# Convolution accumulators in four one-bank buffers, two convolution channels placed sooner, one convolution moved from GpSimd to TensorE, and whole low parts on GpSimd in the first FFN

## The chip, the cores and the metric

The kernel runs on one NeuronCore of one Trainium2 chip. Five engines with an instruction stream each work side by side: TensorE (PE; its weight loads are listed apart as PEld), VectorE (DVE), ScalarE (ACT), GpSimd (POOL) and SyncE (SP), which issues most of the DMAs. The metric is the time of one execution on the device in microseconds. Three executions of the kernel before took 1547.32 to 1551.12 us, with 1550.37 us as median.

## The reference

One step of a streaming encoder on 640 tokens: 512 frames of a new stream (the prompt) and 8 running streams with 16 frames each (the sample), width 1024. Layer 0 is a convolution module and a feed-forward network (FFN), layer 1 attention and an FFN. The change touches layer 0 only:

```python
def conv_module(h, hist, g, w_pw1, b_pw1, w_dw, b_dw, ln_g, ln_b, w_pw2, b_pw2):
    a, gate = jnp.split(rms_norm(h, g) @ w_pw1 + b_pw1, 2, axis=-1)
    glu = a * jax.nn.sigmoid(gate)
    full = jnp.concatenate([hist.astype(glu.dtype), glu], axis=1)
    y = lax.conv_general_dilated(
        full, w_dw[:, None, :].astype(full.dtype), window_strides=(1,), padding="VALID",
        dimension_numbers=("NWC", "WIO", "NWC"), feature_group_count=D_MODEL) + b_dw
    y = jax.nn.silu(layer_norm(y, ln_g, ln_b))
    return h + y @ w_pw2 + b_pw2, full[:, -CONV_HIST:]

def swiglu_ffn(h, g, w_in, w_out):
    a, b = jnp.split(rms_norm(h, g) @ w_in, 2, axis=-1)
    return h + (jax.nn.silu(a) * b) @ w_out
```

The convolution is depthwise and 31 wide; the FFN's hidden width is 2816. Everything is float32.

## The kernel before

**Layout.** Channels lie on the 128 partitions, in 8 tiles of 128 channels; below, "channel 6" is the seventh of these tiles. Tokens lie along the free axis, in two groups (`GR`, line 43): group 0 with 256 tokens (128 of the sample and 128 of the prompt) and group 1 with 384 of the prompt. Layer 0 works through the groups one after the other.

**Products.** A float32 product is made from three matmuls (`mm3`, lines 170 to 172): each operand is split into a high part that TensorE takes at full rate and a low part, the rest. `wsplit` (line 128) does it for weights: one DMA brings 128x2048 values to `raw`, ScalarE copies them to `whi` (line 150), and `wlo` = raw − whi is subtracted (line 154) by VectorE for the first columns and GpSimd for the last `pool` quarters of them. `raw`, `whi` and `wlo` have two buffers each, so the copy of one tile's weights waits until the tile two before it has been read by its last matmul. The same split of activations is `xsplit` (lines 159 and 160).

**The convolution** of one channel tile and group runs in one of three ways. `conv` (letter d in the plan): VectorE, 31 instructions (a start at line 434, 30 steps at line 437) that add into an accumulator in PSUM from the pool `w2`; each buffer of the pool spans two banks and holds two channels, and there are two buffers. `conv_pool` (letter q): ScalarE multiplies (line 416), GpSimd adds (line 417), 31 and 30 instructions. `conv_pe_load` and `conv_pe` (letters l and p): the input goes to DRAM and back four times shifted (DMAs sc and x4), and TensorE makes 32 small matmuls (line 469).

**The order.** `PLAN` (line 70) gives the order of the program for the convolution layer. Its letters, each with the group and the channels behind it: a and b are pw1 with the gate (b is group 1), x the norm of group 1, d, q, l and p convolutions, n the LayerNorm with the swish (`conv_ln`), w is pw2, r the norm ahead of the FFN, f one chunk of the FFN for group 0 (six tiles of `ffn_in`, then `ffn_out`), s the output of the convolution's state. From the program, a scheduler makes one list of instructions for each engine; blocks under `high_priority` are placed earlier than where they stand. Each engine then works through its list in that fixed order, and waits where an operand isn't ready. So an instruction that stands early in a list and must wait holds everything behind it.

**What the prediction follows.** n0 is a chain over four engines: sums over channels on GpSimd and TensorE (`colmean`), the mean to all partitions (`spread`, line 216), subtraction on VectorE (line 483), squares on ScalarE (line 179), their sums on GpSimd (line 195) and TensorE (line 204), `rst` (lines 226 and 230), spread, product (line 489), swish (line 491), split into x. Behind it stand pw2 of group 0, four weight tiles of two output tiles each (w0), then two more pw1 tiles, r0 and the FFN's first tiles. The FFN's tiles are called t0, t1, ... here.

Of the kernel before, what the change touches and what calls it, by code (L numbers as in the profile page):

```python
# [8 lines left out]
F32 = mybir.dt.float32  # L9
# [5 lines left out]
P = 128  # L15
# [33 lines left out]
HP = 2000  # L49
# [17 lines left out]
FG = (1, 0)  # L67
SSQ1 = 'ppapappp'
LNO = ((1, 5, 4, 3, 6, 0, 2, 7), (3, 5, 6, 4, 2, 7, 1, 0))
PLAN = ("a0 y a1 a2 a4 x a3 a5 a6 l04 p04 l05 d0213 a7 b0 p05 b1 l07 p07 l06 b2 q00 s0 p06 n0 b3 b4 b5 d145 l13 w0 b7 r0 p13 b6 f q16 s1 d101 d127 n1 f f w1 r1")  # L70
# [7 lines left out]
def tile_trunk(ctx, tc, xT, vecs, hist, w_pw1, w_pw2, w_in0, w_out0, w_in1, w_out1,  # L78
# [3 lines left out]
    cst = ctx.enter_context(tc.tile_pool(name="cst", bufs=1))  # L82
    wp = ctx.enter_context(tc.tile_pool(name="wp", bufs=2))
    w2s = ExitStack()
    w2 = w2s.enter_context(tc.tile_pool(name="w2", bufs=2, space=PSUM))

    uid = [0]
    tps = ExitStack()
# [3 lines left out]
    def nm(s):  # L92
        uid[0] += 1
        return f"{s}_{uid[0]}"
# [1 line left out]
    def mmt(n=512):  # L96
        return mm.tile([P, n], F32, tag="mm", name=nm("mm"))

    sums = [512]

    def w2t():
        return w2.tile([P, 1024 if sums[0] == 512 else 512], F32, tag="w2", name=nm("w2"))

    h = cst.tile([P, KT, NT], F32, name="h", tag="h")

# [67 lines left out]

    last = {}

    def square(s, n, eng="a"):
        q = tp.tile([P, 384], F32, tag="sq", name=nm("sq"))
        if eng == "a":
            nc.scalar.activation(out=q[:, :n], in_=s, func=AF.Square)  # L179
        else:  # L180
            e = nc.vector if eng == "v" else nc.gpsimd
            e.tensor_tensor(out=q[:, :n], in0=s, in1=s, op=ALU.mult)
        return q[:, :n]

    def colmean(st, pieces, n, cut, tag, eng=nc.gpsimd):
        nt = n // P
        srcs = []
        prev = acc = None
        for s in pieces[:cut]:
            if prev is None:  # L190
                prev = s()
                continue
            if acc is None:
                acc = tp.tile([P, 384], F32, tag="acc", name=nm("acc"))
            last["acc"] = eng.tensor_tensor(out=acc[:, :n], in0=prev, in1=s(), op=ALU.add)  # L195
            prev = acc[:, :n]
        if prev is not None:
            srcs.append(lambda: prev)
        srcs += pieces[cut:]
        w, c0 = len(srcs), sums[0]  # L200
        for k, f in enumerate(srcs):
            s = f()
            for t in range(nt):
                last["sum"] = nc.tensor.matmul(st[:, c0 + t * w + k:c0 + 1 + t * w + k], s[:, t * P:(t + 1) * P],
                                               onec, start=True, stop=True)
        r = tp.tile([P, 4], F32, tag=tag, name=nm(tag))
        if w > 1:
            nc.vector.tensor_reduce(out=r[:, :nt],
                                    in_=st[:, c0:c0 + nt * w].rearrange("p (t k) -> p t k", k=w),
                                    op=ALU.add, axis=mybir.AxisListType.X)  # L210
            return r, r[:, :nt]
        return r, st[:, c0:c0 + nt]
# [206 lines left out]

    def conv(cs, g):  # L420
        n = GR[g][1]
        sts = [w2t() for _ in range(0, len(cs), 2)]
        sts = [sts[i // 2][:, i % 2 * 512:i % 2 * 512 + n] for i in range(len(cs))]
        for j in range(W):
            for i, c in enumerate(cs):
                if g == 0:
                    src = gs[:, c, :, j:j + SB]
                    dst = sts[i].rearrange("p (s w) -> p s w", w=SB)
                else:
                    src = gp[:, c, j:j + n]  # L430
                    dst = sts[i]
                wj = dcol(V_DW + c * W + j)
                if j == 0:
                    nc.vector.tensor_scalar(out=dst, in0=src, scalar1=wj, scalar2=col(V_BDW, c),
                                            op0=ALU.mult, op1=ALU.add)
                else:
                    nc.vector.scalar_tensor_tensor(out=dst, in0=src, scalar=wj, in1=dst,  # L437
                                                   op0=ALU.mult, op1=ALU.add)
# [79 lines left out]
    def step(op, arg):  # L518
# [46 lines left out]

    xs = [rms_late(0, None), rms_late(1, None)]
    tps.close()
    at = ExitStack()
    aps = ExitStack()
    am = aps.enter_context(tc.tile_pool(name="am", bufs=2, space=PSUM))  # L570
    mm = aps.enter_context(tc.tile_pool(name="mm1", bufs=2, space=PSUM))

# [302 lines left out]
            proj_o(PO[p])  # L875
    sps.close()
    aps.close()
    w2s.close()
# [4 lines left out]
    sums[0] = 384  # L883
# [22 lines left out]
    def after(ins):  # L906
        return tc.issue_after(ins.ins) if ins is not None else ExitStack()

    def tmp(t):
        return tp.tile([P, 384], F32, tag=t, name=nm(t))[:, 0:HT]  # L910
# [361 lines left out]
```

## Time and profile before

| what | value |
|---|---|
| median of three runs | 1550.37 us |
| profiled execution | 1551.3 us, its span 1549.5 us |
| mean granted TensorE clock | 0.984 of full speed |
| moved by DMA | 199.95 MB, 129 GB/s |
| VectorE's first eight groups hold | wlo 214.0 us, convolution steps of 384 tokens 103.9 us |
| ScalarE's copies of weights (line 150) | 197.7 us |
| GpSimd's part of the low parts (line 154) | 145.7 us |

The profile shows one execution. Its page gives busy time by engine, the chain that ended last, and groups of instructions: line of the kernel, engine, operation, tile written and tiles read, count, then busy time and mean length in ns, then the idle time of the engine ahead of them and what ended it. Times in rows of the trace are microseconds from the start of the span.

### The profile page before, as it was taken

Reading aid. Unit: us, or ns where it says so; the run is one execution under the profiler, and the core shown is the slowest. Engines: PE = TensorE matmul, PEld = TensorE weight load, DVE = VectorE, ACT = ScalarE, POOL = GpSimd, SP = SyncE. Lnnn points to the kernel's source line nnn. Section 1 sums busy time; section 2 is a strip of 40 time slices with the busy share of each in tenths; the row PEclk is TensorE's granted clock in tenths of the full one; section 3 lists DMA queues with packets and bytes.
Section 4 is the critical chain, followed back from the end, with each engine's and each line's share of the span. In section 5 each row is a group of like instructions: output and inputs, shape, how many; then the busy total and the mean of one; then the engine's idle time right before and its main releaser. Section 6 shows DMA issues by size and latency. Waiting matters only on the chain.

```text
span 1549.5 us, 26569 instructions
## 1 busy us (share of the span) xinstructions
PE 1471.7 (95%) x10770; PEld 1398.9 (90%) x10770; DVE 1050.1 (68%) x1863; ACT 662.4 (43%) x1173; POOL 443.8 (29%) x403
## 2 busy tenths in 40 slices
PE   5888998989999999999999999999989999999997
PEld 5878888989999999999988798886989999999997
DVE  6994999988555455457576767566796476476455
ACT  4544454535423323235454445443554244244244
POOL 6865568877501000001321211110411121121110
PEclk9999999999999999999999999998999999999998
DMA  7784434444421333433655545453103213213211
GB/s 236 234 228 142 137 113 159 148 157 153 147 82 55 129 116 129 135 118 126 202 183 201 174 140 205 133 175 114 55 28 109 82 56 109 82 55 109 82 55 68
DMA packets 59658, 199.95 MB, mean 129 GB/s; under 512 B 10128, under 2 KB 22672, under 8 KB 46736
## 3 DMA queue, kind: packets, MB, share of 16 engines
q1 hardware_dynamic: 59248, 197.96, 39.1%
q8 instruction: 84, 1.38, 0.4%
q10 hardware_dynamic: 288, 0.31, 0.1%
q14 instruction: 38, 0.31, 0.1%
HBM read 187.02 MB, written 11.22 MB: 128 GB/s over the span
## 4 chain that ended last, share of the span: by engine, by line
PE 71%; DVE 16%; ACT 3%; issue 3%; DMA 3%; POOL 2%; SPq 0%; POOLq 0%; DVEq 0%; ACTq 0%
PE mm L170 12%; PE mm L172 12%; PE mm L171 12%; PE pb L968 6%; DVE w L437 5%; DVE wlo L154 4%; PE pc L968 4%; PE pa L968 4%; PE pb L170 1%; PE pb L171 1%; PE pb L172 1%; PE pa L172 1%; PE pa L170 1%; PE pc L170 1%; PE pc L172 1%
## 5 line engine op out<-in xcount | busy, mean ns | idle before, releaser
L171 PE MATMUL mm<-x,wlo 128*128 128x256 f32 (+1 forms) x1344 | 416.8, 312 | 15.4 <-DVE wlo L154 14.9
L170 PE MATMUL mm<-x,whi 128*128 128x256 f32 (+1 forms) x1344 | 413.3, 312 | 6.4 <-ACT x L159 3.7
L172 PE MATMUL mm<-x,whi 128*128 128x256 f32 (+1 forms) x1344 | 412.7, 311 | 0.5
L150 ACT ACTIVATE whi<-raw 128x2048 fp32r<-128x2048 f32 (+2 forms) x117 | 197.7, 1694 | 232.6 <-PE mm L172 138.8
L171 PEld LDWEIGHTS mm<-x,wlo 128*128 128x128 f32 x1344 | 257.1, 192 | 18.7 <-DVE wlo L154 17.5
L170 PEld LDWEIGHTS mm<-x,whi 128*128 128x128 f32 x1344 | 254.5, 191 | 11.2 <-ACT x L159 4.1
L172 PEld LDWEIGHTS mm<-x,whi 128*128 128x128 f32 x1344 | 255.1, 191 | 2.9 <-DVE x L160 1.8
L154 DVE TENSOR_TENSOR wlo<-raw,whi 128x2048 fp32r<-128x2048 f32 (+5 forms) x117 | 214.0, 1832 | 62.2 <-ACT whi L150 61.2
L154 POOL TENSOR_TENSOR wlo<-raw,whi 128x1536 fp32r<-128x1536 f32 (+3 forms) x50 | 145.7, 2918 | 69.0 <-ACT whi L150 69.0
L913 POOL TENSOR_TENSOR raw<-raw 128x512 f32<-128x512 f32 x38 | 50.5, 1330 | 332.3 <-DVE raw L913 257.5
L171 PE MATMUL mm<-hid,wlo 128*128 128x256 f32 (+1 forms) x352 | 107.7, 308 | 6.6 <-DVE wlo L154 6.6
L172 PE MATMUL mm<-hid,whi 128*128 128x256 f32 (+1 forms) x352 | 105.8, 307 | 0.2
L170 PE MATMUL mm<-hid,whi 128*128 128x256 f32 (+1 forms) x352 | 104.6, 307 | 0.1
L437 DVE SCALAR_TENSOR_TENSOR w<-gp,dwv,w 128x384 f32<-128x384 f32 x180 | 103.9, 612 | 0.8
L195 POOL TENSOR_TENSOR acc<-sq,sq 128x384 f32<-128x384 f32 (+1 forms) x8 | 8.1, 1006 | 258.2 <-ACT sq L179 258.1
L171 PEld LDWEIGHTS mm<-hid,wlo 128*128 128x128 f32 x352 | 66.0, 188 | 7.8 <-DVE wlo L154 7.8
L417 POOL TENSOR_TENSOR y<-y,cvt 128x256 f32<-128x256 f32 (+1 forms) x60 | 69.3, 1154 | 6.3 <-ACT cvt L416 4.0
L172 PEld LDWEIGHTS mm<-hid,whi 128*128 128x128 f32 x352 | 65.7, 188 | 0.6 <-DVE hid L160 0.6
L159 ACT ACTIVATE whi<-raw 128x1024 fp32r<-128x1024 f32 x38 | 39.4, 1054 | 61.6 <-PE pc L172 18.1
L170 PEld LDWEIGHTS mm<-hid,whi 128*128 128x128 f32 x352 | 65.2, 188 | 0.4 <-ACT hid L159 0.3
L968 PE MATMUL pa<-x0f,whi 128*128 128x320 f32 x228 | 61.2, 316 | 2.5 <-DVE t L913 2.3
L195 POOL TENSOR_TENSOR acc<-acc,sq 128x384 f32<-128x384 f32 (+1 forms) x48 | 52.7, 1097 | 28.9 <-ACT sq L179 27.5
(317 smaller groups left out, 3391.4 us busy)
## 6 DMA issues: line engine op xcount, KB each, us to landing
raw<-in_w_in SPq DMA_DIRECT2D x62, 1024.0 KB
raw<-in_w_out SPq DMA_DIRECT2D x36, 768.0 KB
raw<-in_w_pw SPq DMA_DIRECT2D x22, 1024.0 KB
cache<-in_ck SPq DMA_DIRECT2D x32, 512.0 KB
cache<-in_cv SPq DMA_DIRECT2D x32, 512.0 KB
raw<-in_w_kq SPq DMA_DIRECT2D x8, 1024.0 KB
x<-sc SPq DMA_DIRECT2D x16, 368.0 KB
raw<-in_w_out SPq DMA_DIRECT2D x4, 1024.0 KB
```

The costliest lines, as they stand in the source:

```text
L150: nc.scalar.activation(out=hi[:, a:b], in_=raw[:, a:b], func=AF.Copy)
L154: eng.tensor_tensor(out=lo[:, a:b], in0=raw[:, a:b], in1=hi[:, a:b].bitcast(F32), op=ALU.subtract)
L159: nc.scalar.activation(out=hi, in_=src, func=AF.Copy)
L170: nc.tensor.matmul(ps, wh, xh, start=(i == 0), stop=False)
L171: nc.tensor.matmul(ps, wl, xh, start=False, stop=False)
L172: nc.tensor.matmul(ps, wh, xl, start=False, stop=(i == last))
L195: last["acc"] = eng.tensor_tensor(out=acc[:, :n], in0=prev, in1=s(), op=ALU.add)
L417: nc.gpsimd.tensor_tensor(out=y[g][:, c, :], in0=y[g][:, c, :], in1=pr[:, :n], op=ALU.add)
L437: nc.vector.scalar_tensor_tensor(out=dst, in0=src, scalar=wj, in1=dst, op0=ALU.mult, op1=ALU.add)
L913: ENG[e].tensor_tensor(out=out, in0=a, in1=b, op=op)
L968: nc.tensor.matmul(ps, a[:, c], b[:, k, :], start=(first and k == 0 and i == 0), stop=(k == 3 and i == 2), skip_group_check=not first)
```

## The change

1. The pool `w2` gets four buffers of one bank (512 values) instead of two of two banks, so that each convolved channel has a buffer of its own. Small sums that lay in the second bank now lie at column 384 of the one bank. The pool is closed ahead of the attention, which opens its own of the old shape.
2. Channels 0 and 1 of group 1 (`d101`) are convolved ahead of n0 in the program, where they stood behind s1. Each block of VectorE's convolutions now issues its first instruction after the end of the block before (`issue_after`).
3. `conv_ln` runs under `high_priority`.
4. Channel 6 of group 1 goes from `conv_pool` (q16) to TensorE (l16, p16 around the first FFN chunk).
5. `ffn_in` gives GpSimd all 2048 columns of wlo where it had 1536 (`pool=3`, in the first three chunks); `ffn_out` there stays at three quarters, 1152 of 1536. The other chunks have pool 0 before and after.

```diff
-PLAN = ("... b2 q00 s0 p06 n0 b3 b4 b5 d145 l13 w0 b7 r0 p13 b6 f q16 s1 d101 d127 n1 f f w1 r1")
+PLAN = ("... b2 q00 s0 p06 d101 n0 b3 b4 b5 d145 l13 w0 b7 r0 p13 b6 l16 f p16 s1 d127 n1 f f w1 r1")
...
-    w2 = w2s.enter_context(tc.tile_pool(name="w2", bufs=2, space=PSUM))
+    w2 = w2s.enter_context(tc.tile_pool(name="w2", bufs=4, space=PSUM))
...
-    sums = [512]
+    wide_w2 = [512]
     def w2t():
-        return w2.tile([P, 1024 if sums[0] == 512 else 512], F32, tag="w2", name=nm("w2"))
+        return w2.tile([P, wide_w2[0]], F32, tag="w2", name=nm("w2"))
...
+    def after(ins):
+        return tc.issue_after(ins.ins) if ins is not None else ExitStack()
...
-        w, c0 = len(srcs), sums[0]
+        w, c0 = len(srcs), 384
...
-        wh, wl = wsplit(wsrc[j], 16, P, pool=pool)
+        wh, wl = wsplit(wsrc[j], 16, P, pool=4 if pool else 0)
...
-        sts = [w2t() for _ in range(0, len(cs), 2)]
-        sts = [sts[i // 2][:, i % 2 * 512:i % 2 * 512 + n] for i in range(len(cs))]
+        sts = [w2t()[:, 0:n] for _ in cs]
...
                 if j == 0:
-                    nc.vector.tensor_scalar(out=dst, in0=src, scalar1=wj, scalar2=col(V_BDW, c),
-                                            op0=ALU.mult, op1=ALU.add)
+                    with after(last.get("conv")):
+                        nc.vector.tensor_scalar(out=dst, in0=src, scalar1=wj,
+                                                scalar2=col(V_BDW, c), op0=ALU.mult,
+                                                op1=ALU.add)
...
+        last["conv"] = end
...
         elif op == "n":
-            zs[g] = conv_ln(g)
+            with tc.high_priority(offset=HP):
+                zs[g] = conv_ln(g)
```

The order moves at three places that the prediction speaks of. In the rows, the number behind a tile's name counts the tiles of the program. The first place is VectorE ahead of n0's `rst`. Before, from the subtraction of the mean (y) on; w_213 is a convolution of d145, gp the gated input that a pw1 tile leaves:

```order
L483 TENSOR_TENSOR y_106<-y_106,w_168_1345 128x256 x8
L395 SCALAR_TENSOR_TENSOR gp<-t_204_1562,t_205_1564 128x384
L154 TENSOR_TENSOR wlo_1704<-raw_1702,whi_1703 128x1024
L434 TENSOR_SCALAR w_213_1628<-gp,dwv,vec 128x384
L226 TENSOR_SCALAR rst_1397<-w_171_1370 128x2
```

And now, the last part of it; w_169 and w_170 are d101, whose steps alternate:

```order
L398 SCALAR_TENSOR_TENSOR gp<-t_214_1690,t_215_1692 128x384
L441 SCALAR_TENSOR_TENSOR w_170_1347<-gp,dwv,w_170_1347 128x384
L441 SCALAR_TENSOR_TENSOR w_169_1346<-gp,dwv,w_169_1346 128x384
L154 TENSOR_TENSOR wlo_1831<-raw_1829,whi_1830 128x1024
...
L229 TENSOR_SCALAR rst_1464<-w_174_1437 128x2
...
L494 TENSOR_TENSOR y_106<-y_106,w_174_1437 128x256 x8
```

At the first "..." stand six more steps of d101, at the second five. In all there are 22 steps between d101's two starts and the subtraction of the mean, 21 between that and rst, where there was one start of d145; with them a second gp and a second wlo moved ahead of rst. From rst to the last x tile of r0 VectorE's list has 77 steps and 4 starts, where it had 46 and 2.

The second place is GpSimd at the sums of n0's squares (acc and sq), before and now:

```order
L195 TENSOR_TENSOR acc_1373<-acc_1373,sq_1383 128x256
L154 TENSOR_TENSOR wlo_1704<-raw_1702,whi_1703 128x1024
L195 TENSOR_TENSOR acc_1373<-acc_1373,sq_1386 128x256
L195 TENSOR_TENSOR acc_1373<-acc_1373,sq_1389 128x256
L195 TENSOR_TENSOR acc_1373<-acc_1373,sq_1392 128x256
L230 TENSOR_TENSOR rst_182_1399<-rst_1397,mhalf 128x2
L154 TENSOR_TENSOR wlo_1763<-raw_1761,whi_1762 128x1024
```

```order
L198 TENSOR_TENSOR acc_1440<-acc_1440,sq_1453 128x256
L198 TENSOR_TENSOR acc_1440<-acc_1440,sq_1456 128x256
L154 TENSOR_TENSOR wlo_1831<-raw_1829,whi_1830 128x1024
L198 TENSOR_TENSOR acc_1440<-acc_1440,sq_1459 128x256
L233 TENSOR_TENSOR rst_185_1466<-rst_1464,mhalf 128x2
```

The low part of pw2's second weight tile stood behind rst, and stands ahead of the last add now. On ScalarE its copy, whi_1830, has moved ahead of the last square in the same way.

The third place is TensorE at the end of pw2's first two weight tiles. Before, mm_1709 and mm_1735 (the first tile's two outputs) end here, and mm_1768 (the second tile's) goes on behind them:

```order
L172 MATMUL mm_1709<-x_1403,whi_1703 128x256
L170 MATMUL mm_1735<-x_1403,whi_1703 128x256
L171 MATMUL mm_1735<-x_1403,wlo_1704 128x256
L172 MATMUL mm_1735<-x_1403,whi_1703 128x256
L170 MATMUL mm_1768<-x_1403,whi_1762 128x256
L171 MATMUL mm_1768<-x_1403,wlo_1763 128x256
```

And now; mm_1777 and mm_1803 are the first tile's outputs, mm_1836 and mm_1862 the second's, mm_1895 and mm_1921 the third's:

```order
L172 MATMUL mm_1777<-x_1470,whi_1771 128x256
L172 MATMUL mm_1803<-x_1470,whi_1771 128x256
L172 MATMUL mm_1836<-x_1470,whi_1830 128x256
L172 MATMUL mm_1862<-x_1470,whi_1830 128x256
L170 MATMUL mm_1895<-x_1470,whi_1889 128x256
L170 MATMUL mm_1921<-x_1470,whi_1889 128x256
L170 MATMUL mm_1954<-x_1470,whi_1948 128x256
```

The two weight tiles used to end one after the other, and now end together, by turns to the last x tile. The FFN's first two tiles, t0 and t1, which came one after the other, are interleaved in the same way; and the 32 matmuls of p16 stand at the end of the first chunk, 5 of them in its last output tiles and 27 behind these. No matmul stands between n0's last spread and pw2, before or now.

More of the change, by code (lines that the diff above doesn't have):

```diff
@@ L69 @@
 LNO = ((1, 5, 4, 3, 6, 0, 2, 7), (3, 5, 6, 4, 2, 7, 1, 0))
-PLAN = ("a0 y a1 a2 a4 x a3 a5 a6 l04 p04 l05 d0213 a7 b0 p05 b1 l07 p07 l06 b2 q00 s0 p06 n0 b3 b4 b5 d145 l13 w0 b7 r0 p13 b6 f q16 s1 d101 d127 n1 f f w1 r1")
+PLAN = ("a0 y a1 a2 a4 x a3 a5 a6 l04 p04 l05 d0213 a7 b0 p05 b1 l07 p07 l06 b2 q00 s0 p06 d101 n0 b3 b4 b5 d145 l13 w0 b7 r0 p13 b6 l16 f p16 s1 d127 n1 f f w1 r1")
 V_NCONV, V_BPW1, V_BDW, V_LNG, V_LNB, V_BPW2 = 0, 8, 24, 32, 40, 48
@@ L433, in conv @@
                 if j == 0:
-                    nc.vector.tensor_scalar(out=dst, in0=src, scalar1=wj, scalar2=col(V_BDW, c),
-                                            op0=ALU.mult, op1=ALU.add)
-                else:
-                    nc.vector.scalar_tensor_tensor(out=dst, in0=src, scalar=wj, in1=dst,
-                                                   op0=ALU.mult, op1=ALU.add)
+                    with after(last.get("conv")):
+                        nc.vector.tensor_scalar(out=dst, in0=src, scalar1=wj,
+                                                scalar2=col(V_BDW, c), op0=ALU.mult,
+                                                op1=ALU.add)
+                else:
+                    end = nc.vector.scalar_tensor_tensor(out=dst, in0=src, scalar=wj, in1=dst,
+                                                         op0=ALU.mult, op1=ALU.add)
+        last["conv"] = end
         for i, c in enumerate(cs):
@@ L567, in tile_trunk @@
     tps.close()
+    w2s.close()
     at = ExitStack()
     aps = ExitStack()
+    w2 = aps.enter_context(tc.tile_pool(name="w2a", bufs=2, space=PSUM))
+    wide_w2[0] = 1024
     am = aps.enter_context(tc.tile_pool(name="am", bufs=2, space=PSUM))
@@ L877, in tile_trunk @@
     aps.close()
-    w2s.close()
+    wide_w2[0] = 512
     hf = ExitStack()
@@ L882, in tile_trunk @@
     w2 = hf.enter_context(tc.tile_pool(name="w2f", bufs=2, space=PSUM, **tr))
-    sums[0] = 384
     mm = hf.enter_context(tc.tile_pool(name="mm2", bufs=2, space=PSUM, **tr))
@@ L904, in tile_trunk @@
     xp = hf.enter_context(tc.tile_pool(name="xp", bufs=1, **tr))
-    def after(ins):
-        return tc.issue_after(ins.ins) if ins is not None else ExitStack()
     def tmp(t):
```

## The prediction

> **What bounds the kernel now.** I read the head of the page first, then its chain, then TensorE's waits, then 20-us windows, and last single rows.
>
> ```profile
> PE 1471.7 (95%) x10770; PEld 1398.9 (90%) x10770; DVE 1050.1 (68%) x1863; ACT 662.4 (43%) x1173; POOL 443.8 (29%) x403
> PE 71%; DVE 16%; ACT 3%; issue 3%; DMA 3%; POOL 2%; SPq 0%; POOLq 0%; DVEq 0%; ACTq 0%
> L171 PE MATMUL mm<-x,wlo 128*128 128x256 f32 (+1 forms) x1344 | 416.8, 312 | 15.4 <-DVE wlo L154 14.9
> L417 POOL TENSOR_TENSOR y<-y,cvt 128x256 f32<-128x256 f32 (+1 forms) x60 | 69.3, 1154 | 6.3 <-ACT cvt L416 4.0
> ```
>
> TensorE is busy 95% of the span, so only its idle time of 1549.5 − 1471.7 = 77.8 us can be won, plus the time lost at half clock. The next view (TensorE's waits from 60 to 400 us, then busy time of each engine by window: PE, PEld, DVE, ACT, POOL, granted clock, DMA share, GB/s) shows where it sits.
>
> ```profile
> PE mm L171 <- DVE wlo L154: 21.6, 18, 3.6
> PE mm L469 <- DMA x<-sc: 10.5, 2, 5.4
> 120.00:140.00 20.00, 20.00 (x150) 19.07 (x143) 8.31 (x14) 6.42 (x12) 8.99 (x9) 1.00 0.45 130
> 140.00:160.00 20.00, 15.87 (x88) 15.13 (x87) 12.59 (x26) 12.99 (x22) 10.79 (x9) 0.83 0.40 141
> 160.00:180.00 20.00, 18.18 (x160) 17.98 (x159) 19.72 (x31) 10.04 (x14) 12.10 (x8) 1.00 0.31 106
> 200.00:220.00 20.00, 17.79 (x126) 17.39 (x125) 20.00 (x35) 10.94 (x19) 11.65 (x6) 0.91 0.29 66
> 400.00:1549.00 1149.00, 1126.16 (x8054) 1073.53 (x8053) 704.74 (x1325) 465.92 (x883) 162.83 (x192) 0.99 0.34 114
> ```
>
> After 400 us TensorE has 22.8 us idle in 1149, and the change leaves the work there as it is. All is decided before 400 us. There VectorE is nearly full from 160 us on, and has free time only in 120 to 160: 11.7 + 7.4 us. That is where the change puts d101, 2 × 31 instructions.
>
> **The change part by part.** *d101 ahead of n0.* First the durations, and the chain that starts pw2 of group 0 (start, length, engine, line; in brackets the idle time before and what ended it).
>
> ```profile
> 119.08 1.01 DVE L437 SCALAR_TENSOR_TENSOR w<-gs,dwv,w 128x256 f32<-128x256 f32 x2
> 132.56 0.16 DVE L208 TENSOR_REDUCE mst<-w 128x2 f32<-128x4 f32 x1 [0.42 <-PE w L204]
> 133.38 2.29 DVE L154 TENSOR_TENSOR wlo<-raw,whi 128x2048 fp32r<-128x2048 f32 x1 [0.46 <-ACT whi L150]
> 137.01 2.74 DVE L483 TENSOR_TENSOR y<-y,w 128x256 f32<-128x256 f32 x8 [1.34 <-PE w L216]
> 141.27 1.08 DVE L395 SCALAR_TENSOR_TENSOR gp<-t,t 128x384 f32<-128x384 f32 x1 [1.52 <-ACT t L380]
> 143.07 1.23 DVE L154 TENSOR_TENSOR wlo<-raw,whi 128x1024 fp32r<-128x1024 f32 x1 [0.72 <-ACT whi L150]
> 149.59 0.16 DVE L226 TENSOR_SCALAR rst<-w 128x2 f32<-128x2 f32 x1 [4.70 <-PE w L204]
> 150.93 0.71 PE L216 MATMUL w<-ident,rst 128*128 128x128 f32 x4 [1.38 <-POOL rst L230]
> 154.28 0.58 PE L170 MATMUL mm<-x,whi 128*128 128x256 f32 x1 [2.64 <-ACT x L159]
> 212.56 2.71 DVE L437 SCALAR_TENSOR_TENSOR w<-gp,dwv,w 128x384 f32<-128x384 f32 x5
> ```
>
> VectorE waited 4.70 us for rst's sums, so it was early; the rows of order show that it will now be late. One convolution step costs 2.71 / 5 = 0.54 us. d0213 ends near 120.1. From there to the reduction stand 2 starts, 15 steps, a gp and a 2048-column wlo: 1.3 + 8.1 + 0.6 + 2.3 = 12.3 us, so the reduction still comes at about 132.6. Behind it stand 7 steps, a gp and the next wlo (3.8 + 0.6 + 2.3, with 0.3 for the two small ones), so the eight subtractions start at about 140, not 137.0, and end near 143. Between them and rst stand 21 steps, two gp and two 1024-column wlo: 11.3 + 1.1 + 2 × 1.23 to 2.4 = 15 to 17 us. rst comes at 158 to 160; I take 158.8. The other legs of the chain are no faster:
>
> ```profile
> 149.62 1.90 ACT L150 ACTIVATE whi<-raw 128x2048 fp32r<-128x2048 f32 x1
> 143.12 3.44 POOL L154 TENSOR_TENSOR wlo<-raw,whi 128x1024 fp32r<-128x1024 f32 x1 [1.18 <-ACT whi L150]
> ```
>
> The whi copy at 149.62 (it must wait for the last pw1 weights to be read) now stands ahead of the last square, and its wlo on GpSimd ahead of the last add: 149.6 + 1.9 + 2.4 to 3.4 + 0.7 gives sums at 155, where they were at 148.9. From rst to the first pw2 matmul it was 154.28 − 149.59 = 4.7 us, now 0.3 more for the five steps behind rst. pw2 starts at 163.8: **+9.5 us**. Nothing covers it, since the order has no other matmul between the spread and pw2.
>
> *pw2 and the first FFN tiles.*
>
> ```profile
> 169.95 0.39 PE L171 MATMUL mm<-x,wlo 128*128 128x256 f32 x1 [1.82 <-DVE wlo L154]
> 192.89 3.03 DVE L154 TENSOR_TENSOR wlo<-raw,whi 128x512 fp32r<-128x512 f32 x1
> 206.42 0.75 DVE L160 TENSOR_TENSOR x<-n,x 128x256 fp32r<-128x256 f32 x2
> 212.69 0.39 PE L171 MATMUL mm<-x,wlo 128*128 128x256 f32 x1 [2.12 <-DVE wlo L154]
> 225.95 0.38 PE L171 MATMUL mm<-x,wlo 128*128 128x256 f32 x1 [0.48 <-DVE wlo L154]
> ```
>
> Before, one of pw2's first two weight pairs was finished some 3 us ahead of the other, so the next copy began early and the wait was 1.82. Now both end together (PE rows of order), so copy and subtraction stand bare: 1.9 + 2.5 = 4.4 us, **+2.6**. A wait of 2.12 was followed by a window at clock 0.91 (0.09 × 20 = 1.8 us lost); so this one costs **+1.7** besides, where the wait of 1.82 had clock 1.00. That makes +13.8. VectorE goes the same way by its own count: from rst to the last x tile of r0 it ran without a gap for 207.2 − 149.7 = 57.4 us with 46 steps; now it has 77 steps and two starts more (0.6 each), and a 1024- and a 512-column wlo fewer (1.2 and 3.0): 57.4 + 31 × 0.54 + 1.2 − 4.2 = 71 us, last x tile at 230. Tiles t0 and t1 of the FFN, interleaved in the new order, end 2 us later at most, at 231 to 232; t0's buffers are free at about 229.7.
>
> *GpSimd takes whole low parts in ffn_in.* The groups by form, and one tile's chain (t3 to t4).
>
> ```profile
> L154 POOL TENSOR_TENSOR wlo<-raw,whi 128x1536 fp32r<-128x1536 f32 x19 | 68.5, 3609 | 29.1 <-ACT whi L150 29.1
> L154 POOL TENSOR_TENSOR wlo<-raw,whi 128x1024 fp32r<-128x1024 f32 x15 | 41.2, 2746 | 28.8 <-ACT whi L150 28.8
> 225.28 1.92 ACT L150 ACTIVATE whi<-raw 128x2048 fp32r<-128x2048 f32 x1 [1.39 <-PE mm L172]
> 227.89 3.52 POOL L154 TENSOR_TENSOR wlo<-raw,whi 128x1536 fp32r<-128x1536 f32 x1
> 230.98 0.97 DVE L154 TENSOR_TENSOR wlo<-raw,whi 128x512 fp32r<-128x512 f32 x1
> 232.01 0.39 PE L171 MATMUL mm<-x,wlo 128*128 128x256 f32 x1 [0.33 <-DVE wlo L154]
> 238.48 0.39 PE L171 MATMUL mm<-x,wlo 128*128 128x256 f32 x1 [0.75 <-DVE wlo L154]
> ```
>
> No row has 2048 columns on GpSimd. The means give 3.61 + (3.61 − 2.75) = 4.5, 4/3 of the larger 4.8, and 3.5 (no dearer than 1536) is the floor; I take 4.55. A tile's weights then need 1.92 + 0.1 + 4.55 = 6.6 us from the release of the buffer; now 232.01 − 225.28 = 6.7, since a convolution add stood before GpSimd and VectorE's part ended last. With two buffers, two tiles take that time plus one tile's own 5.7 (6.06 − 0.33): (6.6 + 5.7) / 2 = 6.15 us each, against 6.06 and 6.47 now. Some 15 tiles at −0.13: **−2**, between −8 (floor) and +3 (4.8 and a stretched start). At t2 nothing hides it: 229.7 + 6.6 = 236.3, an idle wait of 5 us, 1.7 at half clock, and t3 at 236.3 + 5.7 + 1.7 = 243.7, not 225.95: **+17.7** for everything up to there, with 12 to 21 as bounds (rst at 156 or 161 and each wait 1 us off).
>
> *Channel 6 on TensorE.*
>
> ```profile
> 189.68 3.43 PE L469 MATMUL mm<-x,w 128*32 128x384 f32 x40
> 193.69 2.14 PE L469 MATMUL mm<-x,w 128*32 128x384 f32 x24
> 267.49 0.38 PE L171 MATMUL mm<-x,wlo 128*128 128x256 f32 x1 [2.68 <-DVE wlo L154]
> ```
>
> p13 cost 3.43 + 2.14 = 5.6 us. p16 stands where the first chunk ends, mostly in the place of that 2.68 us wait and of the half clock after it (1.7): 5.6 − 2.68 − 1.7 = **+1.2**, 0 to 5.6. The 30 GpSimd adds that go (half of L417's group) cost TensorE only the small waits already counted. l16's transfers stand in SP's queue ahead of t3's weights; TensorE waited 5.4 us for such a pair once; here t3 comes late enough to hide it, and that is the price if not. high_priority on n and issue_after add no instruction. The one-bank accumulators change no shape.
>
> Sum: 17.7 − 2 + 1.2 = +16.9 on the profiled execution's 1551.3: 1568.2. The median of the runs shown is 0.9 lower, so 1567.
>
> **Rivals.** *A, faster:* VectorE's queue was the bound from 160 to 340 us, and 34 us of it now lie in its idle time, so the 21.6 us of waits for wlo go; they do if the subtraction on GpSimd takes about 3.5 us. Then pw2 is late by some 5 us only (VectorE's 19 us of idle time hold most of 23), p16 adds 1.2, and of the waits only 1.8 + 2.1 ahead of t1 stay: 1551.3 + 6.2 − 17.6 = 1540. It decides where rst comes before about 154. Against it stand the counted rows ahead of rst.
>
> *B, no change:* the early loss comes, 17.7, but the waits for wlo behind t3 vanish altogether (21.6 − 1.8 − 2.1 − 2.7 = 15): 1551.3 + 17.7 + 1.2 − 15 = 1555. For it: both engines have less to do there. Against: 4.55 + 1.92 is over 5.7.
>
> *C, worse:* the longer GpSimd work locks VectorE out.
>
> ```profile
> 339.42 3.71 DVE L160 TENSOR_TENSOR hid<-t,hid 128x256 fp32r<-128x256 f32 x1
> 338.85 3.99 POOL L154 TENSOR_TENSOR wlo<-raw,whi 128x1536 fp32r<-128x1536 f32 x1 [2.26 <-ACT whi L150]
> ```
>
> A split of 0.4 us took 3.71 until the subtraction ended, and that one took 3.99 where 3.52 is usual: both lose. At 0.5 us more for each of 15 tiles (7.5) and 1.5 at each of three chunk ends (4.5) it is 1568 + 12 = 1580. The Trainium skill (GPSIMD Engine Reference, Specifications) says that GpSimd's SBUF interfaces are shared with VectorE, in contention with VectorE instructions of two SBUF inputs. The trace agrees (3.71 above), and its convolution steps, whose accumulator is in PSUM, kept 0.54; by that rule all of C would come, by the rows alone only part.
>
> *D, not as said:* d101 could still run late; the order shows it early, so it gets no chance.
>
> **How the numbers follow.** Forecast 0.62, C 0.12, B 0.11, A 0.15. A run of this kernel can tell about 0.3% (4.7 us) from no change. Faster is A, 0.15; same is most of B, 0.1; slower the rest, 0.75. The range takes the forecast's bounds (12 to 21, −8 to +3, 0 to 5.6, not all at one end), C and B: 1548 to 1582.
>
> **What would show it.** In the new trace: rst at 158 to 160 with VectorE busy ahead of it; pw2's first matmul near 163.8; waits of 4 to 5 us ahead of pw2's third group and of t2, each with half clock; whole wlo on GpSimd at 4.55 us, waited for by TensorE every other tile; p16 in a chunk end. It is wrong if rst is before 154, if a convolution step costs clearly less than 0.54, or if tiles go at 5.7.

## The result, and the profile after

The changed kernel takes 1584.97 us (four runs, 1583.73 to 1587.78), the kernel before 1550.22 us in the same comparison: a ratio of 1.023, with a 95% interval of 1.0211 to 1.0249. It is 34.75 us slower, where 1567 was forecast, with 1582 as upper end. The profiled execution has a span of 1583.5 us, 34.0 more than before.

The page of the changed kernel: busy time by engine, the chain by engine, the group of matmuls that waits most.

```profile
PE 1487.2 (94%) x10834; PEld 1406.1 (89%) x10834; DVE 1043.2 (66%) x1845; ACT 647.5 (41%) x1143; POOL 425.6 (27%) x374
PE 74%; DVE 13%; POOL 3%; ACT 3%; DMA 3%; issue 3%; SPq 0%; ACTq 0%; DVEq 0%; POOLq 0%
L171 PE MATMUL mm<-x,wlo 128*128 128x256 f32 (+1 forms) x1344 | 417.7, 313 | 16.4 <-POOL wlo L154 13.3
```

TensorE's idle time grew from 77.8 to 1583.5 − 1487.2 = 96.3 us, and its busy time by 15.5 us: p16 (some 6 us by its rows), and matmuls at half clock. VectorE and GpSimd do less in all, as meant. TensorE's waits from 60 to 450 us, and busy time by window (columns as in the prediction; the last two rows are the end of the changed kernel and the same end of the kernel before):

```profile
PE mm L171 <- POOL wlo L154: 14.0, 10, 3.7
PE w L207 <- POOL acc L198: 6.7, 1, 6.7
PE mm L171 <- DVE wlo L154: 6.2, 5, 2.1
PE mm L170 <- ACT whi L150: 5.4, 4, 1.9
120.00:140.00 20.00, 19.37 (x158) 17.93 (x158) 17.36 (x29) 6.68 (x8) 6.55 (x5) 1.00 0.36 125
140.00:160.00 20.00, 12.41 (x69) 11.99 (x67) 19.00 (x32) 9.44 (x14) 11.83 (x9) 0.85 0.49 147
160.00:180.00 20.00, 15.29 (x100) 14.50 (x100) 19.14 (x45) 8.38 (x19) 0.71 (x1) 0.72 0.09 36
220.00:240.00 20.00, 15.32 (x103) 14.56 (x101) 18.67 (x32) 7.38 (x13) 5.93 (x3) 0.83 0.45 112
240.00:260.00 20.00, 15.40 (x106) 14.71 (x106) 20.00 (x28) 6.62 (x8) 13.42 (x3) 0.83 0.31 107
280.00:300.00 20.00, 19.33 (x176) 14.89 (x175) 3.31 (x7) 6.00 (x5) 15.84 (x5) 1.00 0.48 168
530.10:1583.50 1053.40, 1027.24 (x7374) 973.78 (x7372) 656.07 (x1248) 428.84 (x826) 141.30 (x175) 0.99 0.35 117
500.00:1549.50 1049.50, 1026.16 (x7374) 973.53 (x7372) 655.00 (x1248) 428.55 (x826) 140.19 (x175) 0.99 0.35 117
```

VectorE's free time in 120 to 160 is filled, and from 280 to 300 it has almost nothing to do: its last convolution step of layer 0 ends at 277.6, before at 331.7. TensorE loses its time at 140 to 180 and 220 to 260, by waits and at clocks of 0.72 to 0.85. By the first instruction of the same work in both traces, the delay is 10.8 us at pw2's start (154.28 to 165.12), 16 at the next pw1 tile, 27 at t4 (232.01 to 258.94), 26 to 28 to the end of the second chunk, 33 at the start of the third, 30.1 at the end of layer 0, and 34 at the end.

At n0, VectorE, GpSimd and TensorE (start, length, engine, line; in brackets the idle time before):

```profile
156.35 1.70 POOL L198 TENSOR_TENSOR acc<-acc,sq 128x256 f32<-128x256 f32 x1
158.10 1.01 PE L207 MATMUL w<-onec,acc 128*128 128x1 f32 x4 [6.71 <-POOL acc L198]
157.39 3.23 DVE L441 SCALAR_TENSOR_TENSOR w<-gp,dwv,w 128x384 f32<-128x384 f32 x6
160.54 0.14 DVE L229 TENSOR_SCALAR rst<-w 128x2 f32<-128x2 f32 x1
165.12 0.58 PE L170 MATMUL mm<-x,whi 128*128 128x256 f32 x1 [2.37 <-ACT x L159]
```

Both legs came as worked out: the sums behind the extra wlo on GpSimd (at 158.1, where 155 was forecast), and rst with no idle time on VectorE ahead of it, at 160.5 (158 to 160 was forecast). The next place is r0 and the first FFN tiles:

```profile
223.28 4.53 POOL L154 TENSOR_TENSOR wlo<-raw,whi 128x2048 fp32r<-128x2048 f32 x1 [9.12 <-ACT whi L150]
224.44 4.00 DVE L160 TENSOR_TENSOR x<-n,x 128x256 fp32r<-128x256 f32 x2
230.38 0.58 PE L170 MATMUL mm<-x,whi 128*128 128x256 f32 x1 [1.00 <-ACT x L159]
232.01 0.81 DVE L160 TENSOR_TENSOR x<-n,x 128x256 fp32r<-128x256 f32 x1
239.61 9.23 POOL L154 TENSOR_TENSOR wlo<-raw,whi 128x2048 fp32r<-128x2048 f32 x2 [7.08 <-ACT whi L150]
244.19 0.58 PE L171 MATMUL mm<-x,wlo 128*128 128x256 f32 x1 [1.72 <-POOL wlo L154]
```

Two splits that take 0.75 us took 4.00, until GpSimd's subtraction ended. TensorE then did 60 of t0's and t1's 96 matmuls behind them, those from 230.4 to 236 us at half clock (0.50 granted); it ended them at 239, and t2's weights came at 244. Below, "the lock" is this: a split of VectorE that starts beside a subtraction of GpSimd ends only after it. The same pattern at the change from the second to the third chunk, where n1's x is made:

```profile
362.32 4.54 POOL L154 TENSOR_TENSOR wlo<-raw,whi 128x2048 fp32r<-128x2048 f32 x1 [5.39 <-ACT whi L150]
362.69 5.05 DVE L160 TENSOR_TENSOR x<-n,x 128x384 fp32r<-128x384 f32 x2 [2.20 <-ACT x L159]
367.30 0.71 ACT L496 ACTIVATE n<-y,vec 128x384 f32<-128x384 f32 x1 [3.50 <-DVE x L160]
369.90 1.91 ACT L150 ACTIVATE whi<-raw 128x2048 fp32r<-128x2048 f32 x1
376.46 0.58 PE L171 MATMUL mm<-x,wlo 128*128 128x256 f32 x1 [3.71 <-POOL wlo L154]
```

GpSimd holds VectorE's splits, ScalarE waits 3.5 us for the splits (the tile n that it writes has two buffers), the weights' copy stands behind that n in ScalarE's list, GpSimd waits for the copy, and TensorE for GpSimd. The group of the splits of hid in the FFN, before and after, and GpSimd's new group:

```profile
L160 DVE TENSOR_TENSOR hid<-t,hid 128x256 fp32r<-128x256 f32 x22 | 29.8, 1357 | 1.4 <-ACT hid L159 1.4
L160 DVE TENSOR_TENSOR hid<-t,hid 128x256 fp32r<-128x256 f32 x22 | 52.0, 2365 | 10.5 <-ACT hid L159 10.5
L154 POOL TENSOR_TENSOR wlo<-raw,whi 128x2048 fp32r<-128x2048 f32 x18 | 82.9, 4610 | 46.6 <-ACT whi L150 46.6
```

GpSimd's 2048 columns took 4.61 us (4.55 was forecast); a split took 2.37 us instead of 1.36 in the mean.

### The profile page after: what moved, and what is told of

The parts are those of the page before. It is cut to its first block, busy times and chain, and to the rows that moved or that the text cites. A ratio compares the mean times of both kernels' runs of the same rounds, so it can differ in the third digit from the quotient of the medians.

```text
span 1583.5 us, 26596 instructions
## 1 busy us (share of the span) xinstructions
PE 1487.2 (94%) x10834; PEld 1406.1 (89%) x10834; DVE 1043.2 (66%) x1845; ACT 647.5 (41%) x1143; POOL 425.6 (27%) x374
## 4 chain that ended last, share of the span: by engine, by line
PE 74%; DVE 13%; POOL 3%; ACT 3%; DMA 3%; issue 3%; SPq 0%; ACTq 0%; DVEq 0%; POOLq 0%
PE mm L172 13%; PE mm L171 13%; PE mm L170 13%; PE pb L973 6%; DVE w L441 4%; PE pc L973 4%; PE pa L973 3%; POOL wlo L154 2%; ACT whi L150 2%; DVE wlo L154 2%; PE pb L170 1%; PE pb L172 1%; PE pb L171 1%; PE pa L172 1%; PE pa L170 1%
## 5 line engine op out<-in xcount | busy, mean ns | idle before, releaser
L154 DVE TENSOR_TENSOR wlo<-raw,whi 128x2048 fp32r<-128x2048 f32 (+5 forms) x99 | 176.2, 1783 | 65.1 <-ACT whi L150 63.2
L154 POOL TENSOR_TENSOR wlo<-raw,whi 128x2048 fp32r<-128x2048 f32 (+4 forms) x50 | 166.6, 3338 | 109.7 <-ACT whi L150 107.2
L441 DVE SCALAR_TENSOR_TENSOR w<-gp,dwv,w 128x384 f32<-128x384 f32 x180 | 99.1, 612 | 0.0
L160 DVE TENSOR_TENSOR hid<-t,hid 128x256 fp32r<-128x256 f32 (+1 forms) x44 | 64.2, 1459 | 10.5 <-ACT hid L159 10.5
L142 ACT ACTIVATE whi<-raw,vec 128x128 fp32r<-128x128 f32 (+1 forms) x160 | 52.4, 409 | 17.1 <-PE mm L172 15.4
```

What stands on the lines that cost most here:

```text
L142: nc.scalar.activation(out=hi[:, a:b], in_=raw[:, a:b], func=AF.Copy, scale=gain)
L154: eng.tensor_tensor(out=lo[:, a:b], in0=raw[:, a:b], in1=hi[:, a:b].bitcast(F32), op=ALU.subtract)
L160: nc.vector.tensor_tensor(out=lo, in0=src, in1=hi.bitcast(F32), op=ALU.subtract)
L441: end = nc.vector.scalar_tensor_tensor(out=dst, in0=src, scalar=wj, in1=dst, op0=ALU.mult, op1=ALU.add)
```

## The experiments

Times are medians; ratios are to the kernel before on the same chip, with their 95% intervals.

**1. The division of the low parts.** In the changed kernel, undone, and in two pieces:

```diff
-        wh, wl = wsplit(wsrc[j], 16, P, pool=4 if pool else 0)
+        wh, wl = wsplit(wsrc[j], 16, P, pool=pool)
```

> The changed kernel with ffn_in's low parts divided as before (1536 columns on GpSimd, 512 on VectorE). Theory (two costs: d101 ahead of n0 makes pw2 late by 16 us, and whole low parts on GpSimd lock VectorE's splits for another 12): 1569 to 1577. Rival (all of the loss is VectorE's order, the division is worth nothing, as the prediction had it): 1583 to 1588.

```diff
-                for eng, a, b in ((nc.vector, a, c), (nc.gpsimd, c, b)):
+                m = (c + b) // 2 if pool == 4 else b
+                for eng, a, b in ((nc.vector, a, c), (nc.gpsimd, c, m), (nc.gpsimd, m, b)):
```

> The changed kernel with GpSimd's 2048 columns in two instructions of 1024, so that VectorE can come in between. Theory (VectorE's splits are locked out for the length of one GpSimd instruction, and ScalarE's next copy waits behind them): 1573 to 1581. Rival (GpSimd's own 4.6 us are the cost, whatever their pieces): 1585 to 1590.

Undone: 1570.59 (1.0131, 1.0105 to 1.0157). Two pieces: 1569.32 (1.0124, 1.01 to 1.0148). So some 15 us of the 35 go with either; the second is a little below what its theory had. With two pieces GpSimd's work is the same and its length no less, and yet the time falls by as much: in the changed kernel it is the length of one instruction that costs. The length costs in two ways, and this run takes away both. VectorE's splits wait less (1.53 us in the mean for a split of hid, 2.37 in the changed kernel). And TensorE needn't wait for the whole low part: it takes the columns of the first piece while GpSimd subtracts the second. In the run with two pieces (four pieces for t2 and t3, some 2.4 us each, then the first matmul with a low part; TensorE's waits for wlo from 60 to 450 us):

```profile
237.06 9.76 POOL L155 TENSOR_TENSOR wlo<-raw,whi 128x1024 fp32r<-128x1024 f32 x4 [5.75 <-ACT whi L150]
239.70 0.41 PE L172 MATMUL mm<-x,wlo 128*128 128x256 f32 x1
PE mm L172 <- DVE wlo L155: 5.4, 6, 1.7
PE mm L172 <- POOL wlo L155: 3.1, 4, 1.9
```

The matmul started 0.3 us after the first piece and 2 us ahead of the end of the second; in the changed kernel t2's waited until 244.19, for all of the subtraction that began at 239.61. TensorE's waits for wlo are 8.5 us here, and 14.0 + 6.2 = 20.2 there. How much of the 15 us is the lock and how much TensorE's wait for the whole low part, these two runs don't divide; experiment 5 has the lock without the other.

The same division alone in the kernel before, in one piece and in two:

> The kernel before with nothing changed but ffn_in's low parts, whole on GpSimd. Theory (two costs): 1557 to 1565, with splits of x and hid held for 3 to 5 us beside a subtraction of 4.55. Rival (all of it is VectorE's order): 1546 to 1552. The rival of the prediction in which the waits for wlo vanish: 1535 to 1543.

> The kernel before with whole low parts on GpSimd in ffn_in, in two instructions of 1024 columns (in one it took 1563.4). Theory (the lock of one long instruction is the cost): 1549 to 1556. Rival (in the kernel before GpSimd's own time is the cost, beside its convolution): 1560 to 1567.

One piece: 1563.4 (1.0074, 1.0049 to 1.01). Two: 1563.73 (1.01, 1.0062 to 1.0137). The first is as expected; the second is a miss, for here the two pieces gain nothing (it lies in the rival's range). Its trace (two pieces alone; GpSimd, then TensorE's waits from 340 to 410 us) shows why:

```profile
344.37 4.75 POOL L155 TENSOR_TENSOR wlo<-raw,whi 128x1024 fp32r<-128x1024 f32 x2
349.08 1.19 POOL L418 TENSOR_TENSOR y<-y,cvt 128x384 f32<-128x384 f32 x1
350.24 4.76 POOL L155 TENSOR_TENSOR wlo<-raw,whi 128x1024 fp32r<-128x1024 f32 x2
PE w L205 <- POOL acc L196: 11.0, 1, 11.0
```

The FFN's tiles ran 7 to 13 us ahead of before in the third chunk. But GpSimd was full, and got one add of channel 6 in between two tiles; the convolution of channel 6 ended at 350, n1 was 18 us late (rst at 391.8, before 373.9), and TensorE stood 11 us and then ran at half clock (0.50 granted from 390 to 400 us). So the next two runs move channel 6 too, in both forms:

```diff
-... b6 f q16 s1 d101 d127 ...
+... b6 l16 f p16 s1 d101 d127 ...
```

> The kernel before with whole low parts on GpSimd in two instructions each, and channel 6 on TensorE. Theory (in the run without p16 the FFN tiles were 8 to 12 us ahead, and all of it was lost where n1 waited for channel 6, whose adds GpSimd did too late): n1 comes in time, 1537 to 1545. Rival (GpSimd's own time is the cost): 1558 to 1570, p16's 5 us on top.

> The same with GpSimd's 2048 columns in one instruction. Theory (a late n1 was most of its cost, the lock of one long instruction the rest): 1544 to 1554, 4 to 10 slower than in two pieces. Rival (the lock is nothing): as the run in two pieces, within 2.

Two pieces with p16: 1555.41 (1.0044, 1.0026 to 1.0062); one piece with p16: 1562.68 (1.009, 1.0067 to 1.0112). n1 comes in time now (rst at 365.6 and 347.6), and one piece is 7 us slower than two: with n1 out of the way the length of the instruction shows in the kernel before as well, though both times are above what their theories had. The hope for 1537 to 1545 fell: the tiles were level with before in the first two chunks and only 2 to 7 us ahead in the third. p16 alone:

> The kernel before with channel 6 on TensorE alone. Theory (its 5.6 us stand mostly in a wait, VectorE and GpSimd gain a little): 1549 to 1554. Rival (p16 is the rest of the loss): 1558 to 1566.

1557.08 (1.004, 1.0024 to 1.0057; ten runs), 5.5 us slower and between both expectations. Its one profile has it level with before at the end of layer 0 (+0.4 us) and 4 us behind later, so where the 5.5 us lie isn't settled.

**2. d101's place.** The changed kernel with d101 back behind s1:

```diff
-... s0 p06 d101 n0 ... p16 s1 d127 ...
+... s0 p06 n0 ... p16 s1 d101 d127 ...
```

> The changed kernel with d101 put back behind s1, everything else as changed. Theory (two costs): the 16 us up to b7 go and part of what t0 to t2 lost, the rest stays: 1560 to 1570. Rival (all of it is VectorE's order): 1548 to 1553. pw2's first matmul near 154 by both.

1578.76 (1.0191, 1.0165 to 1.0217): only 6 us less, outside both expectations. n0's rst stood at 150.0, as before, and yet t3 was 16 us late. So a cost of this size sits in a part that neither theory named. Left are the parts that the prediction priced at nothing.

**3. The accumulators.** First alone (with the small sums at column 384 and the pool closed ahead of the attention, as in the change), then with issue_after and the priority (all of the change but d101's place, p16 and the division):

```diff
-    w2 = w2s.enter_context(tc.tile_pool(name="w2", bufs=2, space=PSUM))
+    w2 = w2s.enter_context(tc.tile_pool(name="w2", bufs=4, space=PSUM))
...
-        sts = [w2t() for _ in range(0, len(cs), 2)]
-        sts = [sts[i // 2][:, i % 2 * 512:i % 2 * 512 + n] for i in range(len(cs))]
+        sts = [w2t()[:, 0:n] for _ in cs]
```

> The kernel before with the four one-bank accumulators alone (no issue_after, no priority, old plan, old division). Theory (with a bank for each channel two channels alternate without a stall, so the list of VectorE holds four steps between two x splits of n0 where it held one, 145 steps ahead of r0's rst where it held 124; pw2 and r0 come late): 1557 to 1566, pw2's first add on VectorE 4 to 6 us late. Rival (the buffers are neutral, the rest of the loss in the run with d101 put back is p16): 1548 to 1553.

> The changed kernel with d101 back behind s1, the old division of low parts and channel 6 back on GpSimd: buffers, issue_after and priority are left. Theory (buffers cost): 1556 to 1566, the same as with the buffers alone to 3 us. Rival (p16 is the rest): 1548 to 1553.

1573.27 (1.013, 1.0096 to 1.0164) and 1573.58 (1.0134, 1.0109 to 1.0159): 22 us from the four buffers, more than expected, and nothing that shows from the other two. VectorE between n0's x splits, first in the kernel before, then with the buffers alone:

```profile
158.22 0.61 DVE L437 SCALAR_TENSOR_TENSOR w<-gp,dwv,w 128x384 f32<-128x384 f32 x1
158.74 0.42 DVE L160 TENSOR_TENSOR x<-n,x 128x256 fp32r<-128x256 f32 x1
159.07 0.61 DVE L437 SCALAR_TENSOR_TENSOR w<-gp,dwv,w 128x384 f32<-128x384 f32 x1
```

```profile
160.05 0.74 DVE L160 TENSOR_TENSOR x<-n,x 128x256 fp32r<-128x256 f32 x2
160.72 2.18 DVE L441 SCALAR_TENSOR_TENSOR w<-gp,dwv,w 128x384 f32<-128x384 f32 x4
162.82 0.74 DVE L160 TENSOR_TENSOR x<-n,x 128x256 fp32r<-128x256 f32 x2
163.50 2.18 DVE L441 SCALAR_TENSOR_TENSOR w<-gp,dwv,w 128x384 f32<-128x384 f32 x4
```

Where the kernel before has one step between splits there are four now, since the scheduler has two channels whose steps don't wait for each other. To keep the buffers and take away the alternation, each channel's first step is issued after the end of the channel ahead; first for both groups, then for group 1 alone:

```diff
-        for j in range(W):
-            for i, c in enumerate(cs):
+        for i, c in enumerate(cs):
+            for j in range(W):
...
-        last["conv"] = end
+            last["conv"] = end
```

> The kernel before with the four one-bank accumulators, but each channel's first step issued after the end of the channel ahead of it, so that two channels can't alternate in VectorE's list (127 steps ahead of r0's rst, where the buffers alone have 145 and the kernel before 124; one or two steps between x splits). Theory (the buffers cost by the alternation that they allow, which packs steps ahead of the chain's splits): 1548 to 1557. Rival (the banks or the small sums' new place cost by themselves): 1567 to 1576.

> The kernel before with the four one-bank accumulators, and for group 1 alone each channel's first step issued after the end of the channel ahead (126 steps ahead of r0's rst; d0213 of group 0 as in the run with the buffers alone). Theory (the buffers cost by the alternation of two channels in VectorE's list): 1548 to 1557, n0's rst and t3 both within 4 us of before. Rival (the banks or the chain of two leftovers cost by themselves): 1562 to 1574, with t3 15 us late or more.

1566.16 (1.0121, 1.008 to 1.0162) and 1563.81 (1.0098, 1.0074 to 1.0123). By the times both fall to the rival (the first just below it); the traces split it. In the first, d0213 itself, one channel at a time, ended at 133 instead of 120, and n0 was 9 us late by that alone; from n0 on nothing was added to t3. In the second, everything is within 4 us of before up to the end of the third chunk (rst of n0 −1.2, of r0 +1.1, t3 +2.2), where the buffers alone had +20 at t3 and +28 at the end of that chunk. It loses 10 us later: d101 and d127 end later one after the other, and n1's rst comes at 386.4, 12.5 late. So up to the end of the third chunk the cost of the buffers goes with the alternation, and the banks and the small sums' new place cost nothing that shows; by the time alone, 15 of the 22 us stay. VectorE at the same place in this kernel, and four steps of one channel a little later:

```profile
157.77 0.43 DVE L160 TENSOR_TENSOR x<-n,x 128x256 fp32r<-128x256 f32 x1
158.12 0.62 DVE L445 SCALAR_TENSOR_TENSOR w<-gp,dwv,w 128x384 f32<-128x384 f32 x1
158.64 0.42 DVE L160 TENSOR_TENSOR x<-n,x 128x256 fp32r<-128x256 f32 x1
162.48 2.59 DVE L445 SCALAR_TENSOR_TENSOR w<-gp,dwv,w 128x384 f32<-128x384 f32 x4
```

Counted in VectorE's list, convolution instructions ahead of the last x split of r0, and when that split ended:

```
kernel                              ahead   last x split of r0 ends
before                                142   207.2
four buffers, group 1 in a row        143   208.0
four buffers, issue_after, priority   174   227.8
changed, d101 back behind s1          175   223.4
four buffers alone                    181   231.3
changed, old division, q16            216   230.6
changed, old division                 216   231.1
changed                               219   232.8
changed, without issue_after          239   235.6
```

From 142 to 181 each instruction costs 24.1 / 39 = 0.6 us, the length of one. d101's early place costs much less for as many: 2.8 us for 42 with the old division and q16 (174 to 216), 9.4 us for 44 in the changed kernel (175 to 219). Most of these fill VectorE's free time ahead of n0. In time, d101's place alone, with the old division and q16:

> The changed kernel with the old division of low parts and channel 6 back on GpSimd, so that it differs from the run with buffers, issue_after and priority (1573.6) by d101's early place alone. Theory now (with these buffers the steps are packed ahead of the splits wherever d101 stands; early d101 makes rst 8 us later and the later stages shorter): 1566 to 1575. Rival (early d101 costs what the prediction's sum gave it, and more): 1580 to 1592.

1568.7 (1.0127, 1.0084 to 1.0169), against 1.0134 with d101 late: as expected, and no cost that shows. Its rst of n0 was 8.7 us late against before, and that was made good later. Beside whole low parts and p16 (experiment 2) the same place cost 6 us.

**4. The rest.** Without issue_after, and without the priority, in the changed kernel; and both mends together:

> The changed kernel without issue_after, so that a block of VectorE's convolutions may start before the block ahead of it has ended; order: 144 steps ahead of n0's rst instead of 133, 205 ahead of r0's instead of 184. Theory (steps of convolutions ahead of the chain's own instructions are the cost): 1588 to 1598, rst 5 to 6 us later than with issue_after. Rival (only their sum over the stage counts): 1583 to 1587.

> The changed kernel without high_priority on n (133 convolution steps ahead of n0's rst as with it, 189 ahead of r0's instead of 184). Theory (steps ahead of the chain count at 0.54 us each): 1584 to 1590, r0's rst 2 to 4 us later than in the changed kernel. Rival (the priority is part of the loss): 1575 to 1582.

> The changed kernel with both costs mended: two pieces on GpSimd, and group 1's channels one after the other in VectorE's list. Theory: what is left is d101's early place (131 steps ahead of n0's rst): 1550 to 1560. Rival (early d101 carries the loss): 1565 to 1575.

Without issue_after 1587.08 (1.0228, 1.0195 to 1.0262), without the priority 1583.12 (1.021, 1.0181 to 1.024): neither is clear of the changed kernel (1.0211 to 1.0249), and each lies between its two expectations; 20 more steps ahead of r0's last split moved it by 3 us and the time by less than shows. Both mends 1578.2 (1.0191, 1.0154 to 1.0228), 18 us above the upper end of the theory, above the rival too, and worse than two pieces alone: with d101 early, channels in a row are no fewer ahead of r0's rst (191, as without), but slower, and r0's rst comes at 217.5, where the changed kernel has it at 206.7.

**5. A version that beats both.** What gained elsewhere is the shorter GpSimd instruction. The kernel before, with nothing changed but GpSimd's three quarters in two instructions:

```diff
-                for eng, a, b in ((nc.vector, a, c), (nc.gpsimd, c, b)):
+                m = (c + b) // 2 if pool == 3 else b
+                for eng, a, b in ((nc.vector, a, c), (nc.gpsimd, c, m), (nc.gpsimd, m, b)):
```

> The kernel before with its own division, GpSimd's three quarters (of ffn_in and ffn_out) in two instructions each. Theory of the lock: VectorE's splits get in earlier: 1541 to 1549. Rival (at 3.5 us the lock costs nothing that TensorE sees, and one more instruction's start does): 1550 to 1555.

> The kernel before with its own division, GpSimd's part in two pieces, measured again over more rounds. Theory of the lock (VectorE's splits get in between the pieces): 0.990 to 0.998. Rival (at 3.5 us the lock costs nothing that the time shows): 0.998 to 1.003.

1547.44 (0.9989, 0.997 to 1.0008), and over more rounds 1545.96 (0.9972, 0.9958 to 0.9987; twelve runs): 4 us faster than before; the first comparison alone doesn't tell it from no change. A split of hid takes 1.1 to 1.2 us in the mean in the two profiles, before 1.36, and layer 0 ends 8 and 5 us sooner. VectorE's own quarter of wlo, before and in the first of these runs:

```profile
L154 DVE TENSOR_TENSOR wlo<-raw,whi 128x512 fp32r<-128x512 f32 x23 | 38.2, 1666 | 3.0 <-ACT whi L150 3.0
L155 DVE TENSOR_TENSOR wlo<-raw,whi 128x512 fp32r<-128x512 f32 x23 | 25.6, 1122 | 8.0 <-ACT whi L150 8.0
```

Here TensorE waits for VectorE's quarter, which holds the first columns, and hardly ever for GpSimd's (0.2 us in each of these runs from 60 to 420 us). So GpSimd's earlier first piece is not what it gains: VectorE's quarter took 1.12 instead of 1.67 us, and TensorE's waits for it from 60 to 400 us fell from 21.6 us to 14.1 and 11.9. So what shows here is the lock.

## Why the prediction was wrong

**Where the sum fell short.** The profiled execution is 34.0 us longer, where 16.9 were forecast. 26.9 of them are there at t4 (17.7 forecast), 3.2 come from t4 to the end of layer 0 (−2 + 1.2 forecast), and 3.9 behind layer 0 (nothing forecast). The shortfall is 9.2 + 4.0 + 3.9 us. So two terms failed: t0 to t2, which was mis-sized, and the whole low parts, which had the wrong sign.

**d101 ahead of n0, +9.5: right in size, wrong in cause.** pw2 started 10.8 late by the counted steps, and VectorE's list to r0's last split predicted 230, with 232.8 measured. But the count of 77 against 46 steps from rst to that split was put down to d101. With the four buffers alone there are as many: 86 instructions, starts included, where the changed kernel has 81 and the kernel before 48. What d101 adds stands ahead of rst (138 against 94), and by experiment 3 most of it is absorbed.

**"The one-bank accumulators change no shape", priced at nothing: wrong as a cause.** They cost 22 us by themselves. The instructions are the same, but a tile of its own for each channel makes two chains independent, and the scheduler packs four steps where it placed one. The order was counted rightly; the part of the diff that made it was not asked for. As the sum went by the counted order, it holds this delay under d101's name, so this error isn't what the number lacks; that is luck.

**t0 to t2, +17.7 up to t3: mis-sized by 9.** t4 came 26.9 late. I let t0 and t1 end 2 us behind the last x tile; but 60 of their 96 matmuls were still to do when the split at 224.44 came free, some of them at half clock, so they ended at 239 instead of 231 to 232, and t2 came at 244.2 instead of 236.3. With the old division t0 was hardly earlier (237.1 against 237.8 for its product on VectorE), but t2's product came at 252.1 instead of 257.5. Of these 5.4 us TensorE has 1.4 (the copy that waits for t2's last matmul started at 250.9 instead of 252.3). The rest stands in VectorE's list: in the changed kernel the splits of t0's and t1's hid were held beside two subtractions in a row, and t2's product came behind them and 16 steps with no idle time.

```profile
240.17 4.25 DVE L160 TENSOR_TENSOR hid<-t,hid 128x256 fp32r<-128x256 f32 x1
245.92 3.21 DVE L160 TENSOR_TENSOR hid<-t,hid 128x256 fp32r<-128x256 f32 x1
249.05 8.49 DVE L441 SCALAR_TENSOR_TENSOR w<-gp,dwv,w 128x384 f32<-128x384 f32 x16
257.45 0.41 DVE L291 TENSOR_TENSOR t<-t,mm 128x256 f32<-128x256 f32 x1
```

**Whole low parts, −2: wrong in sign.** Their length was right (4.61). What I set aside as rival C happened: splits waited out the subtraction, most of all at the third chunk (+6 at its start), where ScalarE's copy stood behind the swish that waited for a split. Undoing it gives 14 us. The two-piece runs show that the length of GpSimd's instruction matters, by the lock and, in the changed kernel, by TensorE's later start on the low part as well. The Trainium skill (GPSIMD Engine Reference, Specifications) names exactly this contention, for VectorE instructions of two SBUF inputs; the trace agrees with 5.05 us for two splits beside a 4.54 us subtraction, and with convolution steps that kept 0.54. By that rule as a whole C's 1580 would have been the forecast.

**Channel 6 on TensorE, +1.2:** alone 5.5 in time, at the upper bound of 0 to 5.6. It isn't shown where.

**Rivals.** A's and B's waits for wlo did not go: 20.2 us are left of 21.6, most of them now for GpSimd. A's gain on the tiles exists: with two pieces alone in the kernel before, the third chunk ran 7 to 13 us ahead, until n1 took it back. That p16 is in the change for this is a guess; with it the third chunk was only 2 to 7 us ahead.

**What is left.** "The change leaves the work behind 400 us as it is" holds for the work; yet the stretch from 500 us to the end took 1053.4 us instead of 1049.5; 1.1 us of the difference is busy time of TensorE. The same stretch was between 3.6 us shorter and 4.0 longer in the other profiles, in no order with the parts that they have; runs of the kernel before differ by up to 12 us. It is left open. The parts alone add up to more than the whole: 22 + 13 + 5.5 = 40 against 35.

## What to carry to other kernels

Where a scheduler fills the lists, ask of each buffer that is added which chains it makes independent, and count in the new order what stands ahead of the instructions that another engine waits for: here 39 more steps made r0's last split 24 us later and the kernel 22 us slower. A part that leaves every instruction as it is may still be the costliest.

A long GpSimd subtraction over SBUF held VectorE's splits until its end (0.75 us of splits took 4.00), and through ScalarE's fixed order that came back to GpSimd's own next operand; cut it in pieces before giving it more. And an engine that takes over work in one stage may starve a chain two stages on (GpSimd with channel 6 and n1): look for what else it owes.

## What the runs showed of the hardware

A convolution step of 384 tokens takes 0.61 to 0.62 us by itself. Four of them take 2.18 us (0.54 each) where two channels alternate, so that one starts ahead of the end of the one before, and 2.59 us (0.65 each) where steps of one channel follow each other. So the buffers made VectorE's steps cheaper, and the kernel slower.

The Trainium skill (Trainium Architecture — The Big Picture, What this means for kernel authors) calls the port pair of VectorE and GpSimd an exclusive lock and not a split of bandwidth. The rows agree on VectorE's side: a split of 0.37 us, issued beside a subtraction, ended just after it (224.44 + 4.00 = 228.44 for two, the subtraction at 227.81).
